# Attention queries: split once per pair of heads, their parts copied into double-buffered tiles

## The chip, the cores and the metric

One core of a Trainium2 chip runs the whole program; the other cores are idle. The metric is the device time of one execution in microseconds. The kernel is one launch with all weights in DRAM at its start.

## The reference, cut to what matters

A trunk of two layers works on 512 rows of 1024. Layer 0 mixes with gated linear attention, layer 1 with a sparse attention of 12 heads; each is followed by a convolutional feed-forward. The change concerns the queries of layer 1, which meet three sets of keys (compressed, selected, window):

```python
q, gl, mq = split_cols(xn @ nsa_w_in[0], NSA_SIZES)      # 12 heads of 64
...
qb = q * Dh ** -0.5
s_c = einsum('bgrqd,bgkd->bgrqk', qb, kc) + common_bias(d_c)
s_s = einsum('bgrqd,bgqkd->bgrqk', qb, k_sel) + group_bias(d_s)
s_w = einsum('bgrqd,bgkd->bgrqk', qb, kwb) + common_bias(d_w)
o = gb[..., 0:1] * o_c + gb[..., 1:2] * o_s + gb[..., 2:3] * o_w
```

With 512 rows, the 8 blocks of 64 are all selected and the window reaches back to the first row, so both branches are causal attention over all keys, with one bias by distance.

## The kernel before, in words

**Precision.** A float32 product is made of reduced-precision matmuls: each operand is split into a high part (ScalarE copies it to the type float32r) and a low part (VectorE subtracts the high part from the operand). `split_to` (L297) issues the two instructions. A key tile K holds the high part of a head group's keys in 64 partitions and the low part in the other 64; a query tile holds the same 64 query columns twice, once in each half, so that one matmul over 128 partitions multiplies a query part with both key parts. Two matmuls (high and low query part) make a score. The doubling is done by transfers: `dup` (L403) copies 64 partitions of the source to both halves of the destination, in two transfers from SP's queue.

**The loop.** Heads go in pairs (a and a + 6, a from 0 to 5), and each pair in two steps, for the query tiles of 128 rows (0, 3) and (1, 2). In each of the twelve steps several generators are advanced in turn, six rounds per step:

- `project(a + 2)`: 24 matmuls of 512 columns, two per round, and at the end VectorE writes the scaled queries qf (one buffer) of that pair, so the qf of a pair is complete at the end of the second step of the pair two before it;
- `queries(a + 1)`: duplicates qf into one tile qd for each head of the pair, loads the two bias strips, and splits each qd into tiles Qh and Ql, one buffer each;
- `scores` of the next step: per head three groups of matmuls, then VectorE adds the bias and takes the minimum, ScalarE the exponential, GpSimd the scaling of P by gate and sum;
- `copies`: SP transfers the scaled P to tiles R (type float32r);
- `weights_t`: TensorE transposes R, ScalarE and VectorE copy the transposes to PT;
- `values` of the step before; `compressed(a + 1)`: the branch over compressed keys.

**Order.** TensorE's instructions in the loop are chained by hand in program order (`pe`, L1710). On the other engines and on SP's queue, a planner orders the instructions at build time by when it takes their inputs to be ready, earlier instructions of the program first; the chip then runs each queue in that order. Before the loop, the memory attention (`mem_att`, L493) makes its own query tiles by `stack_q` (L415), from the same pool and tag qd, and `others` (L1850) prepares the first pair in between.

Of the kernel before, what the change touches and what calls it, by code (L numbers as in the profile page):

```python
# [12 lines left out]
F32 = mybir.dt.float32  # L13
FR = mybir.dt.float32r
# [4 lines left out]
S = 512  # L19
# [163 lines left out]
class Trunk:  # L183
# [231 lines left out]
    def stack_q(self, qf, pool, qpool, direct=False):  # L415

        out = []
        for hh in range(2):
            out.append([self.t(pool, [128, S], f"Q{c}{hh}", FR, bufs=1) for c in "hl"])
            if direct:  # L420
                a = slice(64 * hh, 64 * hh + 64)
                for r in (hh, 1 - hh):
                    self.nc.scalar.activation(out[hh][0][64 * r:64 * r + 64], qf[a], AF.Copy)
                    self.nc.vector.tensor_tensor(out=out[hh][1][64 * r:64 * r + 64], in0=qf[a], in1=out[hh][0][a].bitcast(F32), op=ALU.subtract)
                continue
            qd = self.t(qpool, [128, S], "qd", bufs=2)
            self.dup(qd, qf, 64 * hh)
            self.split_to(out[hh][0], out[hh][1], qd)
        return out
# [1121 lines left out]
    def nsa_layer(self):  # L1551
        nc, I, tc = self.nc, self.I, self.tc
        with ExitStack() as outer:
# [11 lines left out]
            with tc.tile_pool(name="nsap", bufs=2) as pp:  # L1565
# [25 lines left out]
                both = self.t(pp, [100, 36], "both", bufs=1)  # L1591
# [44 lines left out]
                for j in range(2):  # L1636
# [44 lines left out]
                    else:  # L1681
# [7 lines left out]
                        for g in range(4):  # L1689
                            hh = g // 2  # L1690
# [11 lines left out]
            qp = outer.enter_context(tc.tile_pool(name="nsaq", bufs=1))  # L1702
            qfs_, Qs, strips, pos, Ps, PTs, scaled = {}, {}, {}, {}, {}, {}, []
# [30 lines left out]

            def queries(a):

                qd = []
                for hh in range(2):
                    qd.append(self.t(qp, [128, S], "qd", bufs=2))
                    self.dup(qd[hh], qfs_[a], 64 * hh)  # L1740
                strips[a], Qs[a] = [], []

                def strip(hh):
                    st = self.t(qp, [128, 896], "strip", bufs=3)
                    src = self.vecd[a + 6 * hh, :]
                    strips[a].append(st)
                    return nc.sync.dma_start(st, bass.AP(tensor=src.tensor, offset=src.offset + 1, ap=[[1, 128], [1, 896]]))

                def parts(hh):
                    Qs[a].append([self.t(qp, [128, S], f"Q{c}{hh}", FR, bufs=1) for c in "hl"])  # L1750
                    self.split_to(Qs[a][hh][0], Qs[a][hh][1], qd[hh])

                if a == 0:
                    yield
                    for hh in range(2):
                        self.behind(strip(hh), self.copied)
                    yield
                    parts(0)
                    parts(1)
                    yield  # L1760
                for hh in range(2 if a else 0):
                    strip(hh)
                    yield
                    parts(hh)
                    yield

            def scores(s):

# [32 lines left out]
            def compressed(a):  # L1801


                qf = qfs_[a]
                pc = self.ps("sc")
                for n in range(4):
                    self.halves(pc[:, 64 * n:64 * n + 64], qf[:, 128 * (3 - n):128 * (4 - n)], kcT[:, a // 3], mm)
                Pc = self.t(wp, [128, 4, 2, 32], "Pc", bufs=1)
                nc.gpsimd.memset(Pc[:, :, :, 31:32], 1e-30)
                for hh in range(2):  # L1810
                    st = strips[a][hh]
                    bias = bass.AP(tensor=st.tensor, offset=st.offset + 864, ap=[st.ap[0], [-128, 4], [-16, 31]])
                    nc.vector.tensor_tensor(out=Pc[:, :, hh, 0:31], in0=pc[:, :256].rearrange("p (n b k) -> p n b k", n=4, b=2)[:, :, hh, 0:31], in1=bias, op=ALU.add)
                Pv = Pc.rearrange("p n b k -> p (n b) k")
                mn = self.t(self.small, [128, 8], "cmn")
                nc.vector.tensor_reduce(out=mn, in_=Pv[:, :, 0:31], op=ALU.min, axis=AX.X)
                nc.vector.tensor_tensor(out=Pv[:, :, 0:31], in0=Pv[:, :, 0:31], in1=mn.unsqueeze(2).to_broadcast([128, 8, 31]), op=ALU.subtract)
                nc.scalar.activation(Pv[:, :, 0:31], Pv[:, :, 0:31], AF.Exp, scale=-1.0)
                yield
                nc.gpsimd.tensor_tensor(out=Pv[:, 6:8, :], in0=Pv[:, 6:8, :], in1=cmask.unsqueeze(1).to_broadcast([128, 2, 32]), op=ALU.mult)  # L1820
                f = self.t(self.small, [128, 8], "cf")
                nc.vector.tensor_reduce(out=f, in_=Pv, op=ALU.add, axis=AX.X)
                nc.vector.reciprocal(f, f)
                g = bass.AP(tensor=gates.tensor, offset=gates.offset + 108 + 3 * a, ap=[gates.ap[0], [-36, 4], [18, 2]])
                nc.gpsimd.tensor_tensor(out=f.rearrange("p (n b) -> p n b", n=4), in0=f.rearrange("p (n b) -> p n b", n=4), in1=g, op=ALU.mult)
                nc.gpsimd.tensor_tensor(out=Pv, in0=Pv, in1=f.unsqueeze(2).to_broadcast([128, 8, 32]), op=ALU.mult)
                yield
                pt = self.ps("pt")
                for n in range(4):
                    tr(pt[:64, 128 * (3 - n):128 * (4 - n)], Pc[:, n, :, :], self.ident)  # L1830
                nc.scalar.activation(PcTs[a % 2][:64], pt[:64, :], AF.Copy)
                nc.vector.tensor_tensor(out=PcTs[a % 2][64:], in0=pt[:64, :], in1=PcTs[a % 2][:64].bitcast(F32), op=ALU.subtract)
                yield

            run = lambda g, n=1: [next(g, None) for _ in range(n)]

            with ExitStack() as ms:
# [6 lines left out]
                def values():  # L1844
                    pv = [self.ps("acc" if t < 2 else "po") for t in range(4)]
                    yield from self.stepsB("nsav", 0, 2, 512, pv, self.x, GKV)
                    for t in range(4):
                        nc.scalar.activation(V[:, t], pv[t].rearrange("p (a d) -> p a d", d=64), AF.Copy, scale=rc[:, t:t + 1])
# [22 lines left out]
                c = compressed(0)  # L1871
# [7 lines left out]
            with tc.tile_pool(name="nsac", bufs=2) as cp:  # L1879
# [68 lines left out]
                for s, (a, qts) in enumerate(steps):  # L1948
                    ahead = scores(s + 1) if s < 11 else iter(())
                    before = values(s - 1) if s else iter(())  # L1950
                    if qts[0] == 0:
                        proj = project(a + 2) if a < 4 else iter(())
                        q = queries(a + 1) if a < 5 else iter(())
                        run(q)
                    for i in range(6):
                        if i == 4:
                            run(before)
                        if a < 5 and i == 4:
                            if qts[0] == 0:
                                run(q)  # L1960
                                run(q)
                            else:
                                c = compressed(a + 1)
                                run(c)
                        if a < 5 and i == 1 and qts[0]:
                            run(q, 2)
                        run(ahead)
                        if s or i > 1:
                            run(now)
                        copies()  # L1970
                        run(proj, 2)
                        if i == 0:
                            run(c)
                    if 8 <= s < 11:
                        main[s - 8] = self.split(o[s - 8], self.xp, [128, S], "x")
                        self.behind(self.made, turned[True])
                        self.behind(self.left, turned[False])
# [13 lines left out]


def build(arrays, index):
    nc = bacc.Bacc("TRN2", target_bir_lowering=False, num_devices=1)
    I = {n: nc.dram_tensor(f"in_{n}", a.shape, mybir.dt.from_np(a.dtype), kind="ExternalInput").ap() for n, a in arrays.items()}
    out = nc.dram_tensor("out", (S, D), F32, kind="ExternalOutput").ap()
    with tile.TileContext(nc) as tc, ExitStack() as ctx:
        Trunk(nc, tc, ctx, I, out, index).build()
    return nc
# [7 lines left out]
```

## Time and profile before

| | us |
|---|---|
| median of 3 runs | 1223.89 (1223.47 to 1224.72) |
| the profiled execution | 1224.9 |
| its span | 1223.1 |
| TensorE busy | 1211.6 (99%) |
| VectorE / ScalarE / GpSimd busy | 912.5 / 729.7 / 275.2 |

A span goes from the first to the last instruction; the execution's own time has 1.8 us around it. TensorE's granted clock is 0.998 of full speed. The attention loop lies roughly between 697 and 829 us. In lists of waits the engine named first is the one that waited; "R<-P" is a transfer into tile R from tile P. Matmuls overlap: a 512-column matmul is recorded with 0.39 us and its successor starts 0.23 us later, so waits are read from start to start.

### The profile page before, as it was taken

What the parts mean: (1) busy time and instruction counts of PE and PEld (TensorE: products, weight loads), DVE (VectorE), ACT (ScalarE), POOL (GpSimd) and SP (SyncE); (2) the same over time, 40 slices, a digit from 0 to 9 for tenths busy, and PEclk for the clock granted to TensorE, in tenths of its full rate; (3) what the DMA queues carried; (4) which work ended last, traced back from release to release, by engine and by line L of the source; (5) the groups of instructions that cost most, each with busy time, mean ns of one, the idle gap of its engine ahead of it and who ended that gap; (6) DMA issues with size and microseconds to landing.
All of it is one profiled execution on the core that took longest, in us unless ns stands there. A gap on an engine that the chain in (4) does not pass through costs nothing.

```text
span 1223.1 us, 22059 instructions
## 1 busy us (share of the span) xinstructions
PE 1211.6 (99%) x8321; PEld 1077.9 (88%) x8321; DVE 912.5 (75%) x1637; ACT 729.7 (60%) x1459; POOL 275.2 (23%) x290
## 2 busy tenths in 40 slices
PE   9999999999999999999999999999999999999997
PEld 8887889889999998888888878878899999998887
DVE  7667886698888889644776878875788888889431
ACT  7656655467666667333544677764576666675331
POOL 1000000014444420000003366660034444400000
PEclk9999999999999999999999999999999999999999
DMA  7541113236666652323725467643256666633221
GB/s 262 155 138 60 36 36 104 103 101 171 158 157 156 156 128 86 125 87 109 210 104 172 125 207 234 206 166 121 72 144 163 157 156 156 156 104 108 103 69 69
DMA packets 59776, 163.09 MB, mean 133 GB/s; under 512 B 7309, under 2 KB 13384, under 8 KB 59670
## 3 DMA queue, kind: packets, MB, share of 16 engines
q1 hardware_dynamic: 47638, 140.66, 34.0%
q0 software_dynamic: 10944, 19.93, 10.7%
q8 instruction: 65, 1.06, 0.4%
q10 hardware_dynamic: 1088, 1.10, 0.3%
q14 instruction: 41, 0.34, 0.1%
HBM read 116.13 MB, written 2.15 MB: 97 GB/s over the span
## 4 chain that ended last, share of the span: by engine, by line
PE 94%; DVE 2%; issue 1%; ACT 1%; DMA 1%; POOL 1%; POOLq 0%; DVEq 0%; ACTq 0%
PE pt L1186 18%; PE acc L326 10%; PE po L1186 9%; PE acc L1419 7%; PE acc L1003 6%; PE po L1358 5%; PE sc L1358 5%; PE sc L1186 5%; PE po L346 3%; PE acc L789 3%; PE po L1717 3%; PE acc L1717 2%; PE acc L1482 2%; PE acc L1623 2%; PE acc L346 2%; PE sc L1717 1%
## 5 line engine op out<-in xcount | busy, mean ns | idle before, releaser
L287 ACT ACTIVATE wh<-wraw 128x1024 fp32r<-128x1024 f32 (+1 forms) x105 | 109.4, 1043 | 140.6 <-PE sc L1358 29.6
L288 DVE TENSOR_TENSOR wl<-wraw,wh 128x1024 fp32r<-128x1024 f32 (+1 forms) x105 | 128.7, 1227 | 74.8 <-ACT wh L287 74.0
L1175 DVE TENSOR_TENSOR wl<-wraw,wh 128x1024 fp32r<-128x1024 f32 x76 | 72.6, 955 | 7.0 <-ACT wh L1172 7.0
L326 PE MATMUL acc<-xh,wh 128*128 128x512 f32 x184 | 72.6, 395 | 0.0
L326 PE MATMUL acc<-xl,wh 128*128 128x512 f32 x184 | 71.9, 391 | 0.0
L326 PE MATMUL acc<-xh,wl 128*128 128x512 f32 x184 | 71.9, 391 | 0.0
L1419 PE MATMUL acc<-a,wh 128*128 128x512 f32 x228 | 71.1, 389 | 0.0
L1166 POOL DMA_DIRECT2D wraw<-rbw x38 | 33.4, 879 | 153.3 <-DVE wl L1175 113.9
L1175 DVE TENSOR_TENSOR wl<-rbw,wh 128x1024 fp32r<-128x1024 f32 x38 | 46.5, 1225 | 26.5 <-ACT wh L1172 26.5
L1056 DVE SCALAR_TENSOR_TENSOR hc<-acc,ntap,hc 128x511 f32<-128x511 f32 x76 | 56.9, 749 | 10.0 <-ACT hc L1053 8.0
L1172 ACT ACTIVATE wh<-wraw 128x1024 fp32r<-128x1024 f32 x76 | 63.9, 843 | 0.6 <-DMA wraw<-rbw 0.5
L1797 POOL TENSOR_TENSOR P<-P,ssm 128x256 f32<-128x256 f32 (+3 forms) x48 | 61.8, 1309 | 1.9
L1056 DVE SCALAR_TENSOR_TENSOR hc<-acc,vec,hc 128x511 f32<-128x511 f32 x76 | 56.9, 749 | 3.0 <-ACT hc L1053 1.7
L1789 ACT ACTIVATE P<-P,smn 128x128 f32<-128x128 f32 (+3 forms) x96 | 53.3, 558 | 7.5 <-DVE smn L1787 6.9
L1161 POOL TENSOR_TENSOR rbw<-s,rbw 128x512 f32<-128x512 f32 x36 | 47.8, 1329 | 36.8 <-DVE xh L1064 19.0
L1358 PE MATMUL po<-a,wh 128*128 128x512 f32 x144 | 56.0, 389 | 0.0
L1358 PE MATMUL sc<-a,wh 128*128 128x512 f32 x144 | 56.0, 389 | 0.0
L1172 ACT ACTIVATE wh<-rbw 128x1024 fp32r<-128x1024 f32 x38 | 40.2, 1059 | 23.4 <-issue 20.5
L1419 PEld LDWEIGHTS acc<-a,wh 128*128 128x128 f32 x228 | 42.8, 188 | 8.9
L1155 POOL TENSOR_TENSOR s<-wraw,rbw 128x512 f32<-128x512 f32 x34 | 44.8, 1317 | 21.4 <-DVE wl L1175 21.4
L1172 ACT ACTIVATE wh<-s 128x512 fp32r<-128x512 f32 x38 | 24.0, 632 | 42.1 <-PE pt L1186 42.1
L1419 PE MATMUL acc<-a,wl 128*128 128x512 f32 x114 | 44.3, 389 | 0.0
(726 smaller groups left out, 4338.7 us busy)
## 6 DMA issues: line engine op xcount, KB each, us to landing
wraw<-in_wp SPq DMA_DIRECT2D x156, 512.0 KB, 3.2
rbw<-in_wp SPq DMA_DIRECT2D x38, 512.0 KB, 4.4
rbw<-rbw POOLq DMA_DIRECT2D x38, 256.0 KB, 4.2
wraw<-rbw POOLq DMA_DIRECT2D x38, 256.0 KB, 3.3
R<-P SPq DMA_DIRECT2D x12, 512.0 KB, 3.3
strip<-vecd SPq DMA_DIRECT2D x12, 448.0 KB, 5.6
R<-P SPq DMA_DIRECT2D x11, 384.0 KB, 3.3
qd<-qf SPq DMA_DIRECT2D x24, 128.0 KB, 3.2
```

Of the source, the lines that this page charges most:

```text
L287: self.made = nc.scalar.activation(wh, raw, AF.Copy)
L288: self.left = nc.vector.tensor_tensor(out=wl, in0=raw, in1=wh.bitcast(F32), op=ALU.subtract)
L326: self.last = self.nc.tensor.matmul(ps[:M, :N], u[:, M * k:M * k + M], x[k][i][:, :N], start=n == 0, stop=n == 23)
L1003: self.nc.tensor.matmul(ps[:, cols], a[:, o], b[:, cols], start=start and i == 0 and k == ks[0], stop=stop and k == 5 and i == 2)
L1056: return [nc.vector.scalar_tensor_tensor(out=c[:, 2 - i:], in0=u[:, :S - 2 + i], scalar=tap(half, j, i, neg), in1=c[:, 2 - i:], op0=ALU.mu ...
L1172: return after("A", nc.scalar.activation(out, x, AF.Copy))
L1175: return after("D", nc.vector.tensor_tensor(out=out, in0=x, in1=hi.bitcast(F32), op=ALU.subtract))
L1186: after("P", nc.tensor.matmul(bank[:, :256], w[:, o], x, start=start and k + i == 0, stop=k == 3 and i == 2, skip_group_check=True))
L1358: after("P", nc.tensor.matmul(first[m], a[:, o], x, start=r + i == 0, stop=r == NJ - 1 and i == 2))
L1419: nc.tensor.matmul(ps, a[:, o], x, start=n == 0, stop=n == 3 * NJ - 1)
L1717: mm = lambda *args, **kw: pe(nc.tensor.matmul(*args, **kw))
L1797: nc.gpsimd.tensor_tensor(out=P, in0=P, in1=f[:, i, :].unsqueeze(2).to_broadcast([128, 2, 128 * t + 128]), op=ALU.mult)
```

## The change

Each pair's qf is split once, into the two parts of one tile qd; the transfers then copy both parts of a head's 64 rows to that head's tile Q, which has two buffers. `stack_q` takes one tile for the duplicates of both heads. [...]

```diff
@@ stack_q
-            qd = self.t(qpool, [128, S], "qd", bufs=2)
+            if not hh:
+                both = self.t(qpool, [128, 2, S], "qd", bufs=1)
+            qd = both[:, hh]
             self.dup(qd, qf, 64 * hh)
             self.split_to(out[hh][0], out[hh][1], qd)
@@ queries
-                qd = []
-                for hh in range(2):
-                    qd.append(self.t(qp, [128, S], "qd", bufs=2))
-                    self.dup(qd[hh], qfs_[a], 64 * hh)
+                qd = self.t(qp, [128, 2, S], "qd", FR, bufs=1)
+                self.split_to(qd[:, 0], qd[:, 1], qfs_[a])
                 strips[a], Qs[a] = [], []
...
                 def parts(hh):
-                    Qs[a].append([self.t(qp, [128, S], f"Q{c}{hh}", FR, bufs=1) for c in "hl"])
-                    self.split_to(Qs[a][hh][0], Qs[a][hh][1], qd[hh])
-
-                if a == 0:
-                    yield
+                    Q = self.t(qp, [128, 2, S], f"Q{hh}", FR, bufs=2)
+                    self.dup(Q.bitcast(F32), qd.bitcast(F32), 64 * hh)
+                    Qs[a].append([Q[:, c] for c in range(2)])
+
+                if a:
+                    strip(0)
+                yield
+                parts(0)
+                parts(1)
+                if not a:
                     for hh in range(2):
                         self.behind(strip(hh), self.copied)
-                    yield
-                    parts(0)
-                    parts(1)
-                    yield
-                for hh in range(2 if a else 0):
-                    strip(hh)
-                    yield
-                    parts(hh)
-                    yield
+                yield
+                if a:
+                    strip(1)
+                yield
@@ the loop over steps
-                        if a < 5 and i == 4:
-                            if qts[0] == 0:
-                                run(q)
-                                run(q)
-                            else:
-                                c = compressed(a + 1)
-                                run(c)
-                        if a < 5 and i == 1 and qts[0]:
-                            run(q, 2)
+                        if a < 5 and i == 4 and qts[0]:
+                            c = compressed(a + 1)
+                            run(c)
+                        if i in (1, 4) and not qts[0]:
+                            run(q)
@@ build
-    nc = bacc.Bacc("TRN2", target_bir_lowering=False, num_devices=1)
+    nc = bacc.Bacc("TRN2", target_bir_lowering=False, num_devices=1, dynamic_dma_scratch_size=8192)
```

## Rows read from the trace of the kernel before

**Rows 1.** The page's table of engines: busy time, share of the span, instructions.

```profile
PE 1211.6 (99%) x8321; PEld 1077.9 (88%) x8321; DVE 912.5 (75%) x1637; ACT 729.7 (60%) x1459; POOL 275.2 (23%) x290
```

**Rows 2.** TensorE's waits between 690 and 830 us, the attention loop: who waited for whom, us in total, times, longest.

```profile
PE sc L1717 <- DVE Ql L302: 1.1, 2, 0.8
PE pt L1718 <- DMA R<-P: 0.8, 2, 0.6
PE pt L1718 <- ACT PT L1913: 0.8, 1, 0.8
```

**Rows 3.** The instructions on tile qd over the whole span: duration in ns as min/median/max, first and last start, form.

```profile
L406 SPq DMA_DIRECT2D qd<-qf x24: 467/588/1472, 678.6 to 795.4; - x24
L301 ACT ACTIVATE Qh<-qd x16: 614/632/642, 662.5 to 798.5; 128x512 fp32r<-128x512 f32 x16
L302 DVE TENSOR_TENSOR Ql<-qd,Qh x16: 665/693/1853, 663.1 to 800.9; 128x512 fp32r<-128x512 f32 x16
```

**Rows 4.** TensorE's timeline at its waits in the loop: start, duration, line, operation; in brackets the recorded idle time before it and what ended it.

```profile
715.07 0.28 PE L1717 MATMUL sc<-K,Ql 128*128 128x256 f32 x1
715.63 0.51 PE L1718 MATMUL pt<-ident,R 128*128 128x128 f32 x4 [0.28 <-DMA R<-P]
...
719.10 0.28 PE L1717 MATMUL sc<-K,Qh 128*128 128x256 f32 x1
719.69 0.39 PE L1717 MATMUL sc<-K,Ql 128*128 128x256 f32 x1 [0.31 <-DVE Ql L302]
...
756.65 0.28 PE L1717 MATMUL sc<-K,Ql 128*128 128x256 f32 x1
757.49 0.52 PE L1718 MATMUL pt<-ident,R 128*128 128x128 f32 x4 [0.56 <-DMA R<-P]
...
798.01 0.39 PE L1003 MATMUL acc<-mo1h,wh 128*128 128x512 f32 x1
798.23 0.40 PE L1003 MATMUL acc<-mo1h,wl 128*128 128x512 f32 x1
799.38 0.39 PE L1717 MATMUL sc<-K,Ql 128*128 128x256 f32 x1 [0.75 <-DVE Ql L302]
```

**Rows 5.** The timeline of all engines in one full turn, 769 to 783 us: start, duration, engine, line, operation, count of merged instructions. SPq is the issue of a transfer.

```profile
769.40 0.68 DVE L1732 SCALAR_TENSOR_TENSOR qf<-acc,rb 128x512 f32<-128x512 f32 x1
769.81 0.71 ACT L1789 ACTIVATE P<-P,smn 128x512 f32<-128x512 f32 x1
...
771.18 2.46 POOL L1797 TENSOR_TENSOR P<-P,ssm 128x256 f32<-128x256 f32 x2
...
771.82 2.33 SPq L1894 DMA_DIRECT2D R<-P  x2
...
774.49 1.12 SPq L406 DMA_DIRECT2D qd<-qf  x2
...
775.72 2.92 POOL L1797 TENSOR_TENSOR P<-P,ssm 128x512 f32<-128x512 f32 x2
...
775.82 1.49 DVE L302 TENSOR_TENSOR Ql<-qd,Qh 128x512 fp32r<-128x512 f32 x1 [1.01 <-ACT Qh L301]
...
778.00 0.28 PE L1717 MATMUL sc<-K,Qh 128*128 128x256 f32 x1
778.12 0.28 PE L1717 MATMUL sc<-K,Ql 128*128 128x256 f32 x1
778.24 0.46 PE L1718 MATMUL pt<-ident,R 128*128 128x128 f32 x4
...
779.36 0.69 DVE L302 TENSOR_TENSOR Ql<-qd,Qh 128x512 fp32r<-128x512 f32 x1
...
782.12 0.28 PE L1717 MATMUL sc<-K,Qh 128*128 128x256 f32 x1
```

**Rows 6.** Half-microsecond stretches of the same turn: busy time of each engine (and instructions), granted clock, mean busy share of the DMA engines, GB/s. In the first two only query transfers move, in the third the 512 KB copy into R.

```profile
771.50:772.00 0.50, 0.50 (x5) 0.41 (x4) 0.50 (x4) 0.50 (x3) 0.50 (x2) 1.00 0.89 193
772.00:772.50 0.50, 0.50 (x4) 0.36 (x3) 0.49 (x3) 0.50 (x2) 0.50 (x1) 1.00 0.94 197
775.00:775.50 0.50, 0.50 (x15) 0.50 (x10) 0.00 (x0) 0.50 (x2) 0.50 (x2) 1.00 1.01 393
```

**Rows 7.** Transfers by their time from issue to landing, in us, KB each: the query transfers issued at 728.1 to 728.7, with nothing beside them, and the last of the pair behind R, issued at 775.0.

```profile
qd<-qf SPq DMA_DIRECT2D x2, 128.0 KB, 2.3
...
qd<-qf SPq DMA_DIRECT2D x1, 128.0 KB, 3.1
```

**Rows 8.** The timeline of the last turn in which a next pair is prepared, on VectorE and SP.

```profile
789.99 0.68 DVE L1732 SCALAR_TENSOR_TENSOR qf<-acc,rb 128x512 f32<-128x512 f32 x1
...
792.41 2.33 SPq L1894 DMA_DIRECT2D R<-P  x2
...
794.79 1.41 SPq L406 DMA_DIRECT2D qd<-qf  x2
```

**Rows 9.** The page's DMA issues from GpSimd's queue, all in the feed-forward layers: KB each, us to landing.

```profile
rbw<-rbw POOLq DMA_DIRECT2D x38, 256.0 KB, 4.2
wraw<-rbw POOLq DMA_DIRECT2D x38, 256.0 KB, 3.3
```

## The prediction

> **What bounds the kernel now.** I read the page's table of engines first [rows 1]: TensorE is busy for 99% of the span, VectorE for 75%, ScalarE for 60%. The two engines whose work the change cuts are not the bound, so an instruction less on them is worth nothing by itself; only a wait of TensorE that it removes counts. The list of TensorE's waits, limited to the attention loop, has three entries [rows 2]: on the low parts of the queries (1.1 us in two waits), on the copies R of the weights (0.8 us in two) and on one PSUM copy (0.8 us). These figures are too small, since a matmul's recorded end overlaps the next one's start, so I took the four places from TensorE's timeline and measured from start to start [rows 4]. From a 256-column score to its successor passes 0.12 us where nothing waits (778.00 to 778.12 and on to 778.24 [rows 5]). The queries cost 719.69 - 719.10 - 0.12 = 0.47 us and, after a 512-column matmul (0.22 us, from 798.01 to 798.23), 799.38 - 798.23 - 0.22 = 0.93 us: 1.40 together. R costs 715.63 - 715.07 - 0.12 = 0.44 and 757.49 - 756.65 - 0.12 = 0.72: 1.16 together. So 2.56 us of 1223.1 can be won where the change reaches, and that is the whole prize.
>
> **What is removed.** Of the sixteen splits that the rows count, four belong to the memory attention and stay; of the loop's twelve, six go: six ScalarE copies of 0.63 us and six VectorE subtractions of 0.69 (once 1.85) [rows 3], 3.8 us and at least 4.1 us. They lie beside TensorE's matmuls and are costed at nothing; the cover is TensorE's own work, busy for the whole of each turn. Also removed is the short link from transfer to split to score. In the turn that I follow [rows 5], VectorE stands idle 1.01 us before 775.82 for the high part, then takes 1.49 us for the low part instead of 0.69, ending at 777.31, and the score needs it at 778.00: only 0.7 us of slack. This is the link that breaks at 719 and 798.
>
> **What is added.** The new order for a pair is split, then transfer, then score, and the transfers carry two parts: still four per pair, but 256 KB each instead of 128. Step by step in the same turn [rows 5]: the projection's result qf is ready at 769.40 + 0.68 = 770.08. ScalarE is inside an exponential until 770.52, so the high part ends at 771.15 or later. The low part has two SBUF operands and meets GpSimd's scaling of P, which begins at 771.18 and ends at 773.64. The 1.49 us subtraction at 775.82 also began just after a scaling (775.72); the same operation with GpSimd between two jobs took 0.69 (779.36). So the low part is ready at 771.8 if it gets in first, at about 772.6 if it pays the 0.8 us extra, and as late as 773.64 + 0.69 = 774.3 if it waits out both scalings.
>
> SP then has four transfers to issue. Queued on the same engine are the R copies of the weights: one for 128 KB at 771.82 and one for 512 KB, which waits for GpSimd until 773.64 and leaves SP free at 771.82 + 2.33 = 774.15. Today the second pair of query transfers is placed behind that copy (774.49), and so it is in the last turn [rows 8]. If the split ends after R is ready, or the planner keeps R first, all four transfers stand there.
>
> **What a doubled transfer costs.** Transfers of a half tile alone move 193 and 197 GB/s with the DMA engines 0.89 and 0.94 busy, and R's full-width rows move 393 [rows 6]. The limit is therefore not the issue interval, and I take 200 GB/s for the new ones too: 256 KB more per pair cost 1.3 us. Today the last transfer of a pair behind R is issued at 774.49 + 0.55 = 775.04 and lands 3.1 us later [rows 7], at 778.15. In its place the first head's doubled pair, issued 0.3 us earlier, lands at 778.15 - 0.3 + 1.3 = 779.15. The score needs it at 778.00: TensorE waits 1.15 us where it does not wait today. Bounds: 0 if the longer rows move at R's rate, 1.5 without the earlier issue. I take 1.15, by the half-tile rows, which are the nearest.
>
> [...]
>
> If instead the first head's transfers get ahead of the large R, they land in time, but R's data wait for some of theirs. With R issued about when it is now, after 256 or 512 KB at 200 GB/s, both come within about 0.3 us after their need at 778.00 and 778.24. I cost such a turn at 0.3 us.
>
> **What has cover.** The second head's transfers follow by 2.6 us of data; its first score, at 782.12, comes 4.1 us after the first head's [rows 5], so they are costed at nothing, and 1 us if that gap closes. Two buffers for the Q tiles remove a wait for the last scores of the pair before, which the list of waits does not show: nothing. In the memory attention the two duplicates of a query now share one buffer, so the next block's transfers wait for a subtraction more, about 1 us, behind matmuls of the values projection: nothing. [...]
>
> **The sum.** There are five turns in which the next pair is prepared. I expect three of the four full ones with all transfers behind R (3 x 1.15) and one with the first ahead (0.3). In the last turn qf is ready at 790.67 and matmuls of the output projection fill in until 798.45 [rows 4, 8]; the pair would be issued from 794.5 and land at about 795.1 + 3.1 + 1.3 = 799.5: 1.0 us. That makes 4.8 us of new waits. The old ones go: 1.40 for the queries, and 1.16 for R, which stand right behind the scores that now wait. Net +2.2 us. The profiled execution took 1224.9 us, its span 1223.1 us and 1.8 us around it; it lies 1.0 us above the median of the three runs, 1223.9. So 1227.1 for an execution like it, and **1226.1** for the median, 0.18% more. A measurement of this kernel can tell about 0.2%, 2.4 us, from no change, so this is forecast as no measurable change that leans to slower.
>
> **Rivals.**
> - *Transfers behind R in every turn, little absorbed*: five waits of 1.15 to 1.5 us less the 1.40 us of the queries, +4.4 to +6.1 us, 1228 to 1230. For it: the second pair stands behind R in both turns shown, and qf is ready 3.6 us before R, of which the split alone takes 1.7 us and up to 4.2. Against it: R's own waits would then go as well.
> - *Faster*: the split gets in before GpSimd's scaling and the first head's pair is issued before about 772.2, at most 2.1 us after qf. Then it has landed before R's data start, all 2.56 us go, 1221.3. It decides at a low part that ends before 771.8. For it: ScalarE can take the copy at 770.52. Against it: GpSimd starts 0.03 us after that copy would end.
> - *All four transfers ahead of R*: R waits for 1 MB at 200 GB/s, 5 us. It would land some 2.2 us late in each of four turns; with 1.0 in the last and 1.40 won, +8.4 us, 1232.3.
> - *The transfers are hidden anyway* (the longer rows move at R's rate): waits of 0 in four turns and 0.9 in the last, -1.7 us, 1222.2.
>
> **How the numbers follow.** Forecast 0.45 (its own range 1224 to 1228), waits in every turn 0.20, all four ahead 0.05, hidden anyway 0.18, faster 0.12. The range leaves out the case of all four ahead and the dearest end of the first rival: 1221.2 to 1229.5. Slower by over 0.2% are the first rival, all four ahead and a third of the forecast: 0.40. Faster by over 0.2% is that rival and little else, since its 2.6 us hardly exceed the 2.4: 0.13. Within 0.2% the rest: 0.47.
>
> **What would show it.** In the profile after: twelve splits fewer by six; query transfers of 256 KB at about 200 GB/s; on SP, their place against the 512 KB R; TensorE's wait at the first score of each pair released by a transfer into Q instead of by the low part; and no change outside the loop. The prediction is wrong if TensorE shows no wait on Q, if R becomes the wait, or if time moves in the feed-forward layers.

## The result: slower, outside the predicted range

The changed kernel takes 1235.28 us, the median of 6 executions (1230.29 to 1237.77); the kernel before, on the same chip, 1223.81 (6 executions, 1222.16 to 1224.72). The ratio is 1.0087 with a 95% interval of 1.0073 to 1.0101. The change loses 11.5 us where 2.2 were forecast, and its executions spread over 7.5 us, those of the kernel before over 2.6. The profiled execution of the changed kernel took 1237.73 us, its span 1235.9 us, 12.8 us more than the span of before. L1717 of the kernel before is L1719 here, L1718 is L1720 and L1003 is L1005.

The table of engines (beside [rows 1]) shows six instructions fewer on VectorE and on ScalarE and the same number on TensorE:

```profile
PE 1217.7 (99%) x8321; PEld 1081.2 (87%) x8321; DVE 908.2 (73%) x1631; ACT 728.6 (59%) x1453; POOL 276.4 (22%) x290
```

The list of TensorE's waits, over the whole span (beside [rows 2]), has a new first line. The waits on the low parts and on R are gone:

```profile
PE sc L1719 <- DMA Q<-qd: 8.7, 5, 3.7
```

TensorE's timeline at the five places (beside [rows 4]; start, duration, operation, in brackets the idle time and what ended it):

```profile
715.28 0.40 PE L1719 MATMUL acc<-xl,wh 128*128 128x512 f32 x1
719.35 0.55 PE L1719 MATMUL sc<-K,Q 128*128 128x256 f32 x1 [3.67 <-DMA Q<-qd]
...
741.67 0.40 PE L1719 MATMUL acc<-xl,wh 128*128 128x512 f32 x1
742.63 0.35 PE L1719 MATMUL sc<-K,Q 128*128 128x256 f32 x1 [0.56 <-DMA Q<-qd]
...
763.02 0.40 PE L1719 MATMUL acc<-xl,wh 128*128 128x512 f32 x1
766.39 0.77 PE L1719 MATMUL sc<-K,Q 128*128 128x256 f32 x2 [2.97 <-DMA Q<-qd]
...
789.55 0.40 PE L1719 MATMUL acc<-xl,wh 128*128 128x512 f32 x1
790.46 0.36 PE L1719 MATMUL sc<-K,Q 128*128 128x256 f32 x1 [0.52 <-DMA Q<-qd]
...
811.95 0.40 PE L1005 MATMUL acc<-xh,wl 128*128 128x512 f32 x1
813.33 0.36 PE L1719 MATMUL sc<-K,Q 128*128 128x256 f32 x1 [0.98 <-DMA Q<-qd]
```

From start to start, less 0.23 us for the 512-column matmul, the first scores of the five pairs wait 3.84, 0.73, 3.14, 0.68 and 1.15 us, 9.5 us in all. Less the 2.56 that are won, that is 7.0 of the 12.8 us. The rest is the clock. Stretches of the changed kernel from about the end of the first and of the third wait on (length, TensorE busy and instructions, granted clock, DMA share, GB/s):

```profile
719.00:725.00 6.00, 5.65 (x23) 0.51 0.95 288
...
766.00:773.00 7.00, 6.61 (x27) 0.52 0.70 236
```

After each of the two long waits TensorE runs at about half clock (0.51 and 0.52) for some 6 us: 5.65 x 0.49 + 6.61 x 0.48 = 5.9 us lost. 7.0 + 5.9 = 12.9, against 12.8 measured; a smaller wait on P (0.36 us recorded, at 794.33) is not in the sum, so it is good to about half a microsecond.

What sets the third wait apart from the second and the fourth shows on the DMA queues. The two views are of the stretch from the first query transfer of the third pair to its first score, and of the same stretch of the second pair. Columns of the queues: packets, MB, share of 16 engines; of the transfers: count, size, median us from issue to landing.

```profile
q8 instruction: 1, 0.02, 0.9%
...
Q<-qd SPq DMA_DIRECT2D x4, 256.0 KB, 6.4
```

```profile
q1 hardware_dynamic: 524, 1.46, 76.7%
...
Q<-qd SPq DMA_DIRECT2D x4, 256.0 KB, 4.0
```

Queue q8, of the kind instruction, moves 65 packets of 16 KB (1.06 MB) in the whole run, and TensorE's 8321 matmuls and 8321 weight loads are 65 blocks of 256; that a packet is a fetch of TensorE's code is inferred from this count, and a run below that shifts the code bears it out. In windows of 1 us, q8 shows a packet among the query transfers of the first, third and fifth pair (in the windows from 713, 759 and 806 us), and none in the second and fourth. The first pair has, besides, all four transfers behind the 512 KB copy R; the fifth has a packet and still waits only 1.15 us, which no run explains.

### The profile page after: what moved, and what is told of

It is laid out like the page before. It is cut to its first block, busy times and chain, and to the rows that moved or that the text cites. A ratio compares the mean times of both kernels' runs of the same rounds, so it can differ in the third digit from the quotient of the medians.

```text
span 1235.9 us, 22046 instructions
## 1 busy us (share of the span) xinstructions
PE 1217.7 (99%) x8321; PEld 1081.2 (87%) x8321; DVE 908.2 (73%) x1631; ACT 728.6 (59%) x1453; POOL 276.4 (22%) x290
## 3 DMA queue, kind: packets, MB, share of 16 engines
q8 instruction: 65, 1.06, 0.4%
## 4 chain that ended last, share of the span: by engine, by line
PE 89%; DMA 4%; issue 2%; DVE 2%; ACT 1%; POOL 1%; SPq 1%; POOLq 0%; DVEq 0%; ACTq 0%
PE pt L1188 18%; PE acc L326 10%; PE po L1188 9%; PE acc L1421 7%; PE acc L1005 6%; PE po L1360 5%; PE sc L1360 5%; PE sc L1188 5%; PE acc L791 3%; PE po L346 2%; PE po L1719 2%; DMA Q<-qd 2%; PE acc L1484 2%; PE acc L1625 2%; PE acc L346 2%
## 5 line engine op out<-in xcount | busy, mean ns | idle before, releaser
L1787 DVE CUSTOM_DVE_ANT_0 P<-sc,strip 128x128 f32<-128x128 f32 (+3 forms) x72 | 30.4, 438 | 25.1 <-PE sc L1719 20.6
```

## The experiments

Each kernel was timed against the kernel before on the same chip, whose median was 1224.3 to 1224.7 us in these runs. "Pair" is the order of the five pairs prepared in the loop.

**The ring alone.** One argument, the size of the ring of descriptors, is added to the kernel before:

```
+    nc = bacc.Bacc("TRN2", target_bir_lowering=False, num_devices=1, dynamic_dma_scratch_size=8192)
```

> The kernel before with the smaller ring of descriptors alone. Theory (the ring costs nothing, the loss is in the attention loop): within 0.1% of the kernel before, 1222.5 to 1225, no new wait of TensorE in the feed-forward parts. Rival (part of the 11 us comes from the ring, by transfers of GpSimd that wait for descriptors): 1226 or more, with a wait of TensorE or VectorE on a GpSimd transfer.

Measured: 1223.73 us, ratio 0.9989 (0.998 to 0.9998). The ring costs nothing.

**Half the bytes.**

```
-                    self.dup(Q.bitcast(F32), qd.bitcast(F32), 64 * hh)
-                    Qs[a].append([Q[:, c] for c in range(2)])
+                    self.dup(Q[:, 0].bitcast(F32), qd[:, 0].bitcast(F32), 64 * hh)
+                    Qs[a].append([Q[:, 0] for c in range(2)])
```

> The changed kernel, but each query transfer carries the high part alone (128 KB), and both score products use it, so the low part of the queries is left out of the result. Theory (the doubled bytes make the first score wait): the second transfer of a pair lands within about 3.5 us of its issue, the waits of TensorE on Q fall from 8.7 us to below 2, the granted clock stays at full speed in the loop, 1221 to 1225. Rival (the new order of split, then transfer, then score is what is late, whatever the bytes): waits on Q of 5 us or more remain, 1230 or more.

Measured: 1225.04 us, ratio 0.9999 (0.999 to 1.0008), clock 0.999. The waits of TensorE:

```profile
PE sc L1719 <- DMA Q<-qd: 1.3, 1, 1.3
PE pt L1720 <- DVE mo1l L302: 1.2, 1, 1.2
```

One wait on Q is left, in the last pair. With 128 KB a transfer (the low part of the queries is left out) the order split, then transfer is no slower than the kernel before, so the doubled bytes carry the loss. It is no faster either; a new wait on mo1l, seen below, takes part of what is won.

**Work in place of the wait.** Twelve products are put into each of the two long waits, in the first and the third pair:

```
+                            for i in range(12 if a in (1, 3) and not hh and qt == 0 else 0):
+                                mm(sc, self.identr, K[g][:, 0, :], start=True, stop=True)
```

(a is the pair's number, so these are the first and the third pair prepared in the loop; the expectation's "second and fourth" counts from pair 0.)

> The changed kernel with twelve more 512-column products (about 2.8 us at full clock) into the bank of the first score of the second and fourth pairs, where TensorE stood idle for 3.7 and 3.0 us; the scores overwrite them. Theory (half of the loss is the clock that the idle time lowers): the filled waits leave idle times below 1 us, the granted clock stays at 1.00 through both places, and work that is added costs less than nothing: 5 us less than in the profile of the changed kernel, 1230 to 1233. Rival (the lower clock there has another cause, or costs nothing): clock 0.50 stays for some 5 us after each place, time 1236 to 1238; if the wait grows by what is filled in, 1240.

Measured: 1234.42 us (1233.88 to 1235.52), ratio 1.0076 (1.0061 to 1.0091), clock 0.999 in each of four executions. In the profiled one twelve products take 2.76 us (from 760.10 to the score at 762.86), and the stretches after them, which were at half clock, are now:

```profile
719.00:725.00 6.00, 6.00 (x53) 1.00 0.84 273
...
766.00:773.00 7.00, 7.00 (x82) 1.00 0.72 245
```

5.5 us of added matmuls leave the kernel 0.9 us below the median of the changed one. So the half clock follows the idle time, and it costs time: up to the fourth pair's first score (784.07 against 790.46) the profiled execution is 5.8 us ahead of the changed kernel's, counted from the loop's start (697.04 against 697.60). The time lies 1.4 us above the range that I expected, since 2.5 us of that are lost again behind it, most of them in two places: the fifth pair's wait is 1.74 us instead of 1.15, and TensorE waits 1.43 us for R before 830.79, which it does not in the changed kernel.

**Half a block of code.** 32 tiny products at the start move the blocks in which TensorE's code is fetched (in the trace they are 64 matmuls and 64 weight loads, 128 instructions):

```
+        for _ in range(32):
+            tiny = nc.tensor.matmul(idle[:8, :8], self.ones[:, :8], self.ones[:, :8], start=True, stop=True)
+            self.behind(tiny, last)
+            last = tiny
```

> The changed kernel with 32 tiny products (8 columns) more in the warm-up at the start, which shift the blocks of 256 instructions in which TensorE's code is fetched by half a block; nothing else differs, the order on every other engine is the same. Theory (a pair's transfers land 2 us later when a code fetch falls among them): the slow pairs are no longer the first, third and fifth but the second and fourth, where the first head's second transfer lands after 5 to 6.5 us in place of 4.0 and TensorE waits 2.5 to 3.7 us in place of 0.7; the first and third wait less than 1.5 us. Time 1228 to 1237. Rival (the pairs differ by what lies around them in the loop): the waits stay at 3.9, 0.7, 3.2, 0.7 and 1.2 us.

Measured: 1237.67 us (1236.9 to 1242.4; the profile is of the slowest), ratio 1.0099 (1.0082 to 1.0116). The second, third and fourth pair on TensorE's timeline, then the transfers of the second pair and of the third:

```profile
741.51 0.40 PE L1724 MATMUL acc<-xl,wh 128*128 128x512 f32 x1
745.07 0.76 PE L1724 MATMUL sc<-K,Q 128*128 128x256 f32 x2 [3.16 <-DMA Q<-qd]
...
766.92 0.40 PE L1724 MATMUL acc<-xl,wh 128*128 128x512 f32 x1
768.19 0.48 PE L1724 MATMUL sc<-K,Q 128*128 128x256 f32 x2 [0.87 <-DMA Q<-qd]
...
788.61 0.40 PE L1724 MATMUL acc<-xl,wh 128*128 128x512 f32 x1
791.42 0.47 PE L1724 MATMUL sc<-K,Q 128*128 128x256 f32 x2 [2.42 <-DMA Q<-qd]
```

```profile
q8 instruction: 1, 0.02, 0.7%
...
Q<-qd SPq DMA_DIRECT2D x4, 256.0 KB, 6.6
```

```profile
q1 hardware_dynamic: 535, 1.49, 83.9%
...
Q<-qd SPq DMA_DIRECT2D x4, 256.0 KB, 4.7
```

The long waits have moved to the second and fourth pair (3.33 and 2.58 us), the third waits 1.04, the first and fifth have none on Q. In windows of the trace, q8 now has a packet among the transfers of the second and fourth pair alone. Nothing in the loop was changed but the place of the code in its blocks. So a fetch of code among the transfers makes them land later, here by some 2 us (6.6 against 4.7). The time is 0.7 us above my range; this profile also has waits that the changed kernel's has not, on R (1.97 us, at 819.70), Pc (1.5) and mo1l (1.2), and the two last stand ahead of the first pair's score, so that pair is no test.

**The second head's transfers later.**

```
                 parts(0)
-                parts(1)
...
                 if a:
+                    parts(1)
                     strip(1)
```

> The changed kernel with the second head's two transfers issued one step later; on SP they then stand behind two more copies of the weights, and no other engine's order changes. Theory (transfers of one queue are served in the order of issue, so the second head's cost the first nothing): the first scores of the pairs wait as in the changed kernel, some 0.7 to 1.2 us without a code fetch among the transfers and 2.5 to 3.9 us with one, and the second head's first score may begin to wait, 0 to 2 us a pair; 1234 to 1240. Rival (the second head's transfers share the DMA engines with the first's and delay them): the first scores' waits fall by about 1 us each, 1228 to 1232.

Measured: 1239.68 us (the median of four), ratio 1.0116 (1.0101 to 1.0132); one of the four executions took 4287 us, for which no trace gives a cause. The first head's first score waits not at all in the first pair (717.57, on its place) and 0.58, 2.01, 0.64 and 1.81 us in the others. Where no code is fetched (second and fourth pair) that is a gain of 0.15 and 0.04 us, so there the second head's transfers do not delay the first's. The first pair says nothing on it: waits on Pc and mo1l stand ahead of it, and its transfers have 5.1 us up to the score instead of 2.6. Why the third gains 1.1 us and the fifth loses 0.7 is open. The second head's own late landing costs 1.39 us at its first score in the second pair, and in the first pair, where I had expected 2 us at most, 3.64, followed by half clock:

```profile
725.09 0.77 PE L1719 MATMUL sc<-K,Q 128*128 128x256 f32 x2 [3.47 <-DMA Q<-qd]
```

**The order on SP, three ways.** In the changed kernel the first transfer of a pair goes ahead of the 512 KB copy R in four pairs of five, as SP's timeline shows for the second pair (beside [rows 5]):

```profile
736.11 0.47 SPq L1894 DMA_DIRECT2D R<-P  x1
736.67 0.55 SPq L406 DMA_DIRECT2D Q<-qd  x1
737.96 0.47 SPq L1894 DMA_DIRECT2D R<-P  x1
738.48 2.67 SPq L406 DMA_DIRECT2D Q<-qd  x3
```

Both transfers of the first head ahead of R (weighed is the last copy R):

```
                     self.dup(Q.bitcast(F32), qd.bitcast(F32), 64 * hh)
+                    if a and not hh:
+                        self.behind(self.weighed, self.copied)
```

> The changed kernel with both of the first head's transfers held ahead of the 512 KB copy of the weights. Theory (one queue, served in order): the second transfer is issued 1.3 us earlier, so pairs without a code fetch no longer wait for Q, pairs with one wait 1 to 2.5 us; the copy R, needed 0.24 us after the first score, comes behind 512 KB instead of 256 and TensorE waits for it 0.5 to 1.5 us a pair; 1227 to 1233. Rival (R is not late behind them): no wait on R above 0.5 us, 1224 to 1227.

Measured: 1234.50 us (1230.71 to 1235.2), ratio 1.0079 (1.0062 to 1.0095). The waits in the loop, and the second pair:

```profile
PE pt L1720 <- DMA R<-P: 5.2, 6, 1.3
PE sc L1719 <- DMA Q<-qd: 1.5, 1, 1.5
```

```profile
737.50 0.40 PE L1719 MATMUL sc<-K,Q 128*128 128x256 f32 x2
739.05 0.34 PE L1720 MATMUL pt<-ident,R 128*128 128x128 f32 x2 [1.15 <-DMA R<-P]
```

In the first four pairs the wait on Q becomes a wait on R right behind it, 1.1 to 1.5 us; the fifth, with a fetch, waits on Q. The profile is of the fastest of four executions; the median is 1.5 us above the range that I expected.

Both behind it:

```
-                    self.dup(Q.bitcast(F32), qd.bitcast(F32), 64 * hh)
+                    for r in range(2):
+                        self.copied = nc.sync.dma_start(...)
+                        if a and not hh:
+                            self.behind(self.copied, self.weighed)
```

> The changed kernel with the first head's two transfers held behind the 512 KB copy of the weights on SP in every turn, the case that the prediction held likeliest. Theory (landing counts from the issue of the second transfer, which comes 0.5 us later than in the changed kernel): pairs without a code fetch among the transfers wait 1.1 to 1.4 us, which is what the prediction took, pairs with one 3 to 4.2 us, two or three of them followed by some 5 us of half clock; 1235 to 1241. Rival (the prediction's 1.15 us holds for every pair, and the slow pairs come from the place ahead of the copy): no wait above 1.6 us, clock at full speed, 1226 to 1231.

Measured: 1242.40 us, ratio 1.014 (1.0124 to 1.0155). From the second pair on, the planner put one of the second head's transfers into the place ahead of R, so these pairs have 256 KB more ahead of the first head's. The waits are 2.61, 2.11, 2.91, 2.19 and 1.77 us, and neither theory has them right. In the second and fourth pair they are 1.4 and 1.5 us longer than in the changed kernel: 256 KB in 1.4 us is 187 GB/s, near the rate of [rows 6]. Here the bytes issued ahead on the same queue were waited for in full.

All four behind it (if a: in place of if a and not hh:), the order that the prediction had forecast:

> The changed kernel with all four query transfers of a pair held behind the 512 KB copy of the weights on SP, which is the order that the prediction held likeliest in four of five turns (it was so in the first only). Theory (bytes of one queue served in order, a landing counted from the last byte, a code fetch among them 0.8 to 2.4 us more): ahead of the first head's last byte stand as many bytes as in the changed kernel, the stream starts 0.5 to 0.8 us later, so pairs without a fetch wait 1.1 to 1.6 us and those with one 2 to 4 us; 1232 to 1241. Rival (the prediction as made, 1.15 us in every turn and nothing else): no wait above 1.6 us, no stretch of half clock, 1226 to 1229.

Measured: 1237.19 us (1235.5 to 1239.39), ratio 1.0101 (1.0085 to 1.0118). The second and third pair on TensorE's timeline, and the stretch after the first of these waits:

```profile
739.74 0.40 PE L1719 MATMUL acc<-xl,wh 128*128 128x512 f32 x1
741.79 0.47 PE L1719 MATMUL sc<-K,Q 128*128 128x256 f32 x2 [1.65 <-DMA Q<-qd]
...
763.72 0.40 PE L1719 MATMUL acc<-xl,wh 128*128 128x512 f32 x1
765.86 0.47 PE L1719 MATMUL sc<-K,Q 128*128 128x256 f32 x2 [1.74 <-DMA Q<-qd]
```

```profile
742.00:746.00 4.00, 4.00 (x20) 0.57 1.04 287
```

These two pairs wait 1.82 and 1.91 us, and so does the fourth (1.91), where the prediction took 1.15 and my theory 1.1 to 1.6; a fetch of code at 759 us came before their first query transfer was issued (760.56) and did no harm. The first pair, with a fetch at 711 among its transfers (issued from 711.03), waits 4.56, and the fifth 1.01. Here waits of 1.65 us (as recorded, from end to start) are followed by half clock too. Not every wait of this length is: in the run with both behind, the fourth pair's, recorded with 2.03 us, is followed by a clock of 1.00 (791.2 to 794.6 us), the second's, with 1.94, by 0.50 (743.1 to 746.5).

**No transfers.** ScalarE and VectorE write each head's parts into both halves of its tile, in place of the split of qf and the transfers:

```
+                    own = slice(64 * hh, 64 * hh + 64)
+                    for r in (hh, 1 - hh):
+                        half = slice(64 * r, 64 * r + 64)
+                        nc.scalar.activation(Q[half, 0], qfs_[a][own], AF.Copy)
+                        nc.vector.tensor_tensor(out=Q[half, 1], in0=qfs_[a][own], in1=Q[own, 0].bitcast(F32), op=ALU.subtract)
```

> The changed kernel without query transfers: ScalarE and VectorE write each head's high and low part straight into both halves of its tile, four half-tile copies and four half-tile subtractions a pair; two buffers and the smaller ring stay. Theory (the loss is the landing of the transfers): qf is ready some 7 us before the first score, eight instructions of 0.65 to 0.7 us on two engines side by side take about 3 to 4.5 us of them, no wait of TensorE on Q or on the low part is left, nor R's, which no longer shares the queue: 1221 to 1222.5. Rival (VectorE and ScalarE, with four instructions a pair more than the changed kernel's two splits on each... six more in all, become late with the PSUM copies): waits of TensorE on PT or P of 2 us or more in sum, 1224 to 1227.

Measured: 1234.75 us, ratio 1.0084 (1.0071 to 1.0098), far above what I expected and above the rival too. The waits of TensorE in the loop, and VectorE's row that explains them:

```profile
PE pt L1720 <- ACT PT L1915: 2.1, 5, 0.8
PE sc L1719 <- DVE smn L1789: 1.5, 1, 1.5
```

```profile
734.73 4.09 DVE L1753 TENSOR_TENSOR Q<-qf,Q 64x512 fp32r<-64x512 f32 x4
738.85 0.42 DVE L1789 CUSTOM_DVE_ANT_0 P<-sc,strip 128x256 f32<-128x256 f32 x1
```

Four subtractions in a row hold VectorE for 4.1 us, and the score's reduction waits behind them. No query transfer is waited for, but every turn has small waits on PSUM copies and reductions, and the one of 1.5 us, before 716.46, is followed by half clock (0.50 from 717 to 720.4 us).

**Half of the transfers.** The same, but each part is written once, into the head's own half, and the other half is one transfer of 256 KB:

```
+                for Q, o in zip(Qn, own):
+                    self.split_to(Q[o, 0], Q[o, 1], qfs_[a][o])
...
+                    self.copied = nc.sync.dma_start(Q[own[1 - hh]].bitcast(F32), Q[own[hh]].bitcast(F32))
```

> The changed kernel with each head's own half written in place by ScalarE and VectorE (two half-tile copies and two half-tile subtractions a pair) and only the other half copied by transfer: two transfers of 256 KB a pair in place of four. Theory (bytes in flight ahead of the first score): the first head's single transfer, issued ahead of the 512 KB copy of the weights, lands about 3.2 us after its issue, 2 us more with a code fetch among it; waits on Q below 1.5 us in sum, R's waits of before come back in part: 1221.5 to 1224. Rival (the order split, then transfer, then score is too long by itself): waits on Q of 3 us or more, 1226 or more.

Measured: 1230.62 us (1229.27 to 1231.98), ratio 1.005 (1.0038 to 1.0063). No wait on Q is left, as the theory has it, but the time is the rival's, by waits that neither names: on PSUM copies (3.1 us in five), on R (2.4 in four) and on mo1l (1.2). ScalarE does two copies back to back, 1.27 us from 730.32, ahead of the exponential and the PSUM copies.

**Two buffers alone.** The kernel before with bufs=2 for the query tiles and the smaller ring:

```
-                    Qs[a].append([self.t(qp, [128, S], f"Q{c}{hh}", FR, bufs=1) for c in "hl"])
+                    Qs[a].append([self.t(qp, [128, S], f"Q{c}{hh}", FR, bufs=2) for c in "hl"])
```

> The kernel before with two buffers for the query tiles and the smaller ring that makes room for them; no engine's order changes. Theory (no wait of TensorE or VectorE comes from the single buffer): as with the ring alone, 1223.0 to 1224.5, the two waits on the low parts stay at about 1.4 us. Rival (the low part is late because its tile is still read): both waits go, 1222 or less.

Measured: 1223.89 us, ratio 0.9993 (0.9984 to 1.0002); the two waits on the low parts stay (1.4 us as recorded; 1.1 in [rows 2]). The buffers gain nothing.

**The order of split and transfer undone.** The changed kernel, with the queries copied first and split in each head's tile:

```
-                self.split_to(qd[:, 0], qd[:, 1], qfs_[a])
+                for hh in range(2):
+                    self.dup(qd[:, hh], qfs_[a], 64 * hh)
...
-                    self.dup(Q.bitcast(F32), qd.bitcast(F32), 64 * hh)
+                    self.split_to(Q[:, 0], Q[:, 1], qd[:, hh])
```

> The changed kernel with one part undone: queries are copied to the heads' tiles first (128 KB a transfer, no parts) and split there, as in the kernel before; the new places of the steps, the two buffers and the smaller ring stay. Theory (the order split, then transfer, with its doubled bytes is the whole loss): 1222.5 to 1225.5, no wait on a transfer of queries, waits on the low parts of 0.5 to 2 us in sum. Rival (the new places of the steps or the buffers carry part of the loss): 1227 or more.

Measured: 1223.48 us (1221.88 to 1224.29), ratio 0.9989 (0.998 to 0.9998). All that remains of the change is worth 0.8 us, and the kernel with the ring alone has the same ratio. Nothing tried here beats the kernel before by more than this 0.1%.

## Why the prediction failed, point by point

**What held.** TensorE's wait at the first score of each pair is released by a transfer into Q, transfers of 256 KB move at about 200 GB/s (176 to 205 before the waits of the run with all four behind), the splits in the loop fall from twelve to six, the two buffers and the second head's transfers cost nothing (nor does the ring: 1223.73 us alone), and no time moves outside the loop: the last compressed values products begin at 821.7 us before and at 835.0 after, 401.4 and 400.9 us ahead of the span's end, and until 700 us the clock is 1.00 in both. The split is even quicker than feared: its five low parts in the loop take 0.68 to 0.70 us. One count was off without consequence: [rows 3] leaves out two early splits; over the whole span they are eighteen, six of them of the memory attention.

**The step that failed** is the cost of one turn, in three terms. *First, the place and its price.* I expected three of four full turns with all transfers behind R, and costed a turn with the first transfer ahead at 0.3 us. Four of five have the first one ahead, and that costs 0.7 us where nothing disturbs it. The order that I forecast costs not 1.15 but 1.8 to 1.9, as the run with all four behind shows. By these terms alone the loss would have been 0.73 + 0.68 and about as much in the third, 1.15 in the last and, as an estimate, 1.4 to 2.6 in the first (3.84 less a fetch's 2.4, or the first wait of the run with both behind, which has this order and its fetch ahead of R): 4.7 to 5.9, less 2.56, is 2.1 to 3.3 us, so even without the other two terms the forecast would have come near by luck, by errors that cancel. *Second, the fetch of code,* which the sum did not have. It adds 2.4 us to the third pair (3.14 against 0.7), by the estimate above 1.2 to 2.4 to the first, and nothing that can be told in the fifth. The trace of before had it: here the 512 KB copy R and the second pair of query transfers, in the turn where R is waited for at 757.49 [rows 4] and in the one of [rows 5], from the issue of the transfers to just after the first score.

```profile
q8 instruction: 1, 0.02, 1.1%
...
R<-P SPq DMA_DIRECT2D x1, 512.0 KB, 5.1
...
qd<-qf SPq DMA_DIRECT2D x2, 128.0 KB, 4.9
```

```profile
R<-P SPq DMA_DIRECT2D x1, 512.0 KB, 3.4
qd<-qf SPq DMA_DIRECT2D x2, 128.0 KB, 3.2
```

I read the landing of 3.1 us in the quiet turn [rows 7] as the landing, and did not ask why R, which lands in time in other turns, was late in two. *Third, the clock.* Every term of the sum took a wait of TensorE at its length. 5.9 of the 12.8 us are half clock after the wait. Whether and for how long it comes seems to differ from one execution to the next, which is in line with a mean granted clock of 0.993 in the slowest and 0.998 in the fastest of the six executions. The waits that had it behind them were, as recorded, 3.67 us (then a clock of 0.51), 2.97 (then 0.52) and, in the run with all four behind, 1.65 (then 0.57); what decides whether it comes, no run shows.

**The rivals.** Waits in every turn (1228 to 1230) was the right mechanism with the wrong size. All four ahead of R was not tried; with the first head's two ahead, R is the wait, as that rival has it, but 1.1 to 1.5 us a turn and not 2.2. Hidden anyway is refuted by the waits. Faster is not refuted in its condition: in the second turn the low part did get in just ahead of GpSimd's scaling, and was ready at 735.60. But SP stood on the small copy R until 736.11, and the pair was not ahead of the large one.

**The prize.** No kernel tried won the 2.56 us. With the waits on queries and R nearly gone, the run with the order undone gains 0.8 us, and the one with half the bytes nothing; waits on PSUM copies (1.5 us in two) or on mo1l (1.2) take their place.

## What to carry to other kernels

When work moves from compute engines that have slack to transfers that a score waits for, count the bytes ahead of the last one on the same queue at the rate of a half-width transfer (here about 200 GB/s), and read the landing in the worst turn of the trace, not in the quiet one. Cost a wait of TensorE with the clock behind it, at up to twice its length by what was measured here: the third pair's 3.14 us had 3.2 us lost behind them. Single waits from 1.5 us on had half clock behind them (0.50 in the run without transfers), though some up to 2.03 us had not (1.00 in the run with both behind). Removing instructions from an engine with slack gave nothing here, but adding them at the wrong moment did: the kernel with four in a row on VectorE lost 10 us, the one with two 6 us, R's waits included.

## What the runs showed of the hardware

A fetch of TensorE's code, 16 KB, among the query transfers delayed their landing by about 2 us (4.0 to 6.4 and 4.7 to 6.6 us) in the two kernels above. It is not always so much: in the third pair of the run with the first head's two ahead and of the run with the second head's later, each with a fetch, the second transfer lands after 4.8 and 4.7 us instead of the 4.4 and 3.9 of their second pairs, without one. The fetch comes once in about 256 of TensorE's instructions (65 packets for 16642), so a shift of the code by 128 instructions moved the slow turns. What in the DMA engines causes the delay, and sets its size, no run shows.

The subtraction of the split, where it began while GpSimd scaled, took 2.38 instead of 0.68 us. With the kernel that holds both first transfers ahead of R, GpSimd, VectorE and TensorE show how far that reaches:

```profile
706.24 3.44 POOL L1799 TENSOR_TENSOR P<-P,ssm 128x256 f32<-128x256 f32 x2
```

```profile
707.86 2.38 DVE L302 TENSOR_TENSOR qd<-qf,qd 128x512 fp32r<-128x512 f32 x1
710.16 0.68 DVE L302 TENSOR_TENSOR mo1l<-pt,mo1h 128x512 fp32r<-128x512 f32 x1
```

```profile
710.89 0.28 PE L1720 MATMUL pt<-ident,R 128*128 128x128 f32 x1 [1.20 <-DVE mo1l L302]
```

The split of the first pair stands ahead of mo1l on VectorE, and TensorE waits for mo1l. It is so in the profiles of five of the kernels built on the changed one; in the profile of the changed kernel itself the split began between two scalings (709.36, 0.68 us). What makes it longer beside GpSimd, no run shows.
